# Opening the MLP with plain blocks and keeping its last two pairs on chip

## The chip, the cores and the metric

The kernel runs on one core of one Trainium2 chip. The metric is device time in microseconds (us) of one execution; the time before is 2349.77 us, the median of three runs (2349.01 to 2350.35). Two more figures belong to the one execution that the profiler recorded: its own time, 2352.8 us, and its span, 2351.0 us from the first to the last instruction.

## What is computed

Two encoder layers over 1152 tokens (1024 of a prompt, 8 x 16 of later chunks), width 1024, all in float32. Each layer is a mixer followed by an MLP with a residual:

```python
def channel_mlp(x, w1, w2):
    return jnp.square(jax.nn.relu(x @ w1)) @ w2
...
        yp = yp + mp
        ...
        yp = yp + channel_mlp(rms_norm(yp, ffn_norm_g[layer]), ffn_w1[layer], ffn_w2[layer])
```

`w1` is 1024 x 4096 and `w2` 4096 x 1024. The mixer of layer 0 is attention beside a recurrent branch, that of layer 1 a gated MLP over 128-token chunks; each ends in an output projection of 1024 x 1024 and a residual. The change lies in the MLPs and in the two output projections ahead of them.

## The kernel before

Activations stand with features on the partitions and tokens along the row: eight tiles `x[0]` to `x[7]` of 128 x 1152. TensorE takes float32 in a rounded form, so every operand is split into a high and a low part: ScalarE copies the high part (`split_to` for activations, L390; L189 for weights), VectorE subtracts it from the value (L391, L190). Each product is three matmuls, high-high, high-low, low-high (`product`, L1228, matmul at L1235), on two stretches of 288 tokens.

**The MLP's products** are made from blocks of 2 x 2 with seven products in place of eight (Winograd's form of Strassen's scheme), numbered 1 to 7. In the first product (`first_product`, L1240) a *pair* m, of 16, is the two slabs m and m+16 of `w1`, 128 outputs each; its blocks are the two slabs by the two halves of the inputs (tiles 0-3, 4-7), and the activations are cut into the same halves and into token halves t1 and t2 of 576. One product of a pair is 4 x 2 x 3 = 24 matmuls and is called a *step*. The activations' seven operands `B[1]` to `B[7]` are made once: `B[1]` and `B[2]` are blocks of the first token half as they are, `B[3]` one of the second, and 6, 5, 7, 4 are sums and differences (`other_operands`, L1153). The weights' sums are made pair by pair on VectorE (`Weights.source`, L159), then split into one of 7 slots (`W_SLOTS`), one per step (`W.pump`). Results gather in PSUM banks of the tag `two`, of which there are four, and go by ScalarE or VectorE to rows `c`.

**What follows a pair** goes into the deque `post`, three entries after each step: relu and square on ScalarE, four differences on VectorE (L1261), and seven stores (L1253): each splits one block into a tile `ho` and sends 576 KB to `hidden` in DRAM, since the second product needs its seven operands in split form.

**The second product** (`second_product`, L1325) runs over 8 groups g of two pairs, and for each over two halves q of the outputs, so k = 2g+q counts 0 to 15; each k has 14 steps of 12 matmuls. A group needs 14 tiles `h`, read back from `hidden`; they stand in a ring of 17 slots that also holds three `x` tiles, and group g+1 is loaded as group g is used up. VectorE adds every step's result to `x` (L1352). The residual `x` was put aside in `scratch` by the output projection and is read back at the start (`x_load`, L1076).

**Ahead of the MLP** the output projection (`out_projection`, L1129; `out_bank`, L1091) makes one bank of 128 x 384 at a time, d the output tile and nb the third of the tokens, adds it to `x`, stores it in `scratch`, and sums the squares for the RMS norm with `stat` (L443): ScalarE squares, GpSimd or VectorE adds (L456). The last nine banks are d = 5, 6, 7 for each nb, and the sums are made at those. `normalise` takes the sums over partitions with TensorE (`stat_tokens`, L466), runs the reciprocal root as a chain of small VectorE operations (`rsqrt`, L430), spreads the result with TensorE (`spread_stat`, L476) and scales the eight tiles (`scale`, L1116). For nb = 1 this is called one bank late, after bank (5,2), and followed by the splits of `B[1]` and `B[2]`. For nb = 2 it runs inside the first product, in `last_statistics` and `other_operands`, which then makes all five other operands in one go after the third step.

The first product starts with these steps (m, n); `B[3]` is wanted at the fourth:

```python
        todo = [(0, 1), (0, 2), (1, 1), (0, 3), (1, 2), (0, 6), (0, 5), (1, 3), (0, 7), (1, 6), (0, 4), (1, 5), (2, 1), (1, 7),
                (2, 2), (1, 4)]
```

It ends with pairs 14 and 15 together; then `mlp` (L1383) empties `post`, closes the operands' space, opens the ring, which lies in that space, and only then are the first loads of `h` asked for. All large transfers are issued by SyncE (the rows' SPq), which takes them in its own order. The compiler may set the order of each engine's instructions other than the program does where they do not depend on one another.

Of the kernel before, what the change touches and what calls it, by code (L numbers as in the profile page):

```python
# [19 lines left out]
P = 128  # L20
# [19 lines left out]
W_SLOTS, WX_SLOTS = 7, 5  # L40

PRODUCTS = (1, 2, 4, 6, 5, 7, 3)
H_SLOTS = 17
# [54 lines left out]
class Weights:  # L98
# [5 lines left out]
    def __init__(self, nc, raw_pool, pools, order):  # L104
# [14 lines left out]
        self.raw, self.tiles, self.s2 = {}, {}, None  # L119
# [13 lines left out]
    def _needs(self):  # L133

        last = {}
        for i, (key, n, first, how) in enumerate(self.ops):
            if how is None or n in (1, 2, 7, 3):
                last[first] = i
            if how is not None and n in (4, 5, 6, 3):
                last[first + 1] = i  # L140
        return last
# [17 lines left out]
    def source(self, i):  # L159

        key, n, first, how = self.ops[i]
        if how is None:
            return self.raw[first][:, n * 512:n * 512 + 512]
        r0, r1 = self.raw[first], self.raw.get(first + 1)
        a11, a12 = r0[:, 0:512], r0[:, 512:1024]
        if n in (1, 2, 7):
            return a12 if n == 2 else a11
        v = self.nc.vector
        if n == 3:
            v.tensor_sub(a12, a12, self.s2)  # L170
            return a12
        a21, a22 = r1[:, 0:512], r1[:, 512:1024]
        if n == 6:
            v.tensor_sub(a11, a11, a21)
            v.tensor_add(a21, a21, a22)
            v.tensor_sub(a22, a22, a11)
            self.s2 = a22
        return {4: a22, 6: a22, 5: a21}[n]
# [92 lines left out]
def body(ctx, tc, io):  # L271
# [79 lines left out]
    def add_mlp(l):  # L351
        for m in range(FP):
            order.append((("w1", l, m), [io["w1"][l, m], io["w1"][l, m + FP]], PRODUCTS))
        for g in range(FP // 2):
# [88 lines left out]
    def stat(nb, kt, src, on_dve=False, sum_on_dve=False):  # L443
        if kt == 0:
            s = space["st"].pool.tile([P, NBW], F32, tag="s", bufs=space["sums"], name=f"s{stat.n}")
# [630 lines left out]
    def x_load(d, src, tag=None):  # L1076
        if tag == "h":
            x[d] = space["ring"].pool.tile([P, NTOK], F32, tag="h", bufs=H_SLOTS, name=f"x{d}_{x_load.n}")
# [12 lines left out]
    def out_bank(key, keep, kts=range(KT), ps=None):  # L1091
# [34 lines left out]
    def b_tile(name, n):  # L1126
        B[n] = space[name].pool.tile([P, 2, 4, HT], F32R, name=f"b{n}_{Phase.n}")

    def out_projection(key, keep, gi):  # L1129
# [8 lines left out]
        while todo:  # L1138
            out_bank(key, keep)
            if todo and todo[0] == (6, 1):  # L1140
                normalise(0, gi)
            if todo and todo[0] == (6, 2):
                normalise(1, gi)
                for kt in range(4):
                    b_split(1, kt, x[kt][:, 0:HT])
                for kt in range(4):
                    b_split(2, kt, x[kt + 4][:, 0:HT])
        psum(two=1)

    def last_statistics(gi):  # L1150
        stat_tokens(NB - 1, "two")

    def other_operands(gi):  # L1153

        spread_stat(NB - 1, "two")
        scale(NB - 1, gi)
        for k in sorted((k for k in ("st", "xn0", "xn1")), key=lambda k: -space[k].n):
            space.pop(k).close()
        space["rest"] = Phase("rest")
        for n in (3, 4, 6, 5, 7):  # L1160
            b_tile("rest", n)
        t1, t2 = slice(0, HT), slice(HT, NTOK)
        for kt in range(4):
            b_split(3, kt, x[kt + 4][:, t2])
        for kt in range(4):
            u, v = x[kt], x[kt + 4]
            nc.vector.tensor_sub(u[:, t1], u[:, t2], u[:, t1])
            nc.vector.tensor_sub(u[:, t2], v[:, t2], u[:, t2])
            nc.vector.tensor_sub(v[:, t2], v[:, t2], u[:, t1])
            b_split(6, kt, v[:, t2])  # L1170
        for kt in range(4):
            b_split(5, kt, x[kt][:, t1])
            b_split(7, kt, x[kt][:, t2])
        for kt in range(4):
            v = x[kt + 4]
            nc.vector.tensor_sub(v[:, t1], v[:, t1], v[:, t2])
            b_split(4, kt, v[:, t1])
# [61 lines left out]

    def first_product(l, gi):  # L1240

        rows, bk, post = {}, {}, deque()

        def squares(m, n):
            r = rows[m]
            if n == 0:
                post.append(lambda: nc.scalar.activation(r[0], r[0], AF.Relu))
                post.append(lambda: nc.scalar.square(r[0], r[0]))
            else:
                post.append(lambda: nc.scalar.activation(r[1][:, t2], r[1][:, t2], AF.Relu))  # L1250
                post.append(lambda: nc.scalar.square(r[1], r[1]))

        def store(m, n, src):  # L1253
# [4 lines left out]
            post.append(go)  # L1258

        def less(o, a, b):  # L1260
            post.append(lambda: nc.vector.tensor_sub(o, a, b))  # L1261

        def step(m, n):
            if m not in rows:
                rows[m] = []
                for i, tag in enumerate({0: ("xc", "xb"), 1: ("xb", "xb"), FP - 1: ("xc", "xb")}.get(m, ("xa", "xa"))):
                    pool, bufs = (space["early"].pool, 1) if tag == "xc" else (xp, 4)
                    rows[m].append(pool.tile([P, NTOK], F32, tag=tag, bufs=bufs, name=f"c{l}_{m}_{i}"))
            r = rows[m]
            apart = m < 2  # L1270
            b = {1: "x", 6: "x", 7: "x", 4: "x", 2: "y", 5: "z", 3: "w" if apart else "z"}[n]
            first = n in (1, 2, 5) or (apart and n == 3)
# [7 lines left out]
            o = {1: r[0][:, t1], 2: r[0][:, t1], 6: r[0][:, t2], 3: r[0][:, t2], 5: r[1][:, t2], 7: r[1][:, t2], 4: r[1][:, t1]}[n]  # L1280
            o, ps = halved(o), both(ps)
            if n in (1, 5) or n == (3 if apart else 6):
                nc.scalar.copy(o, ps)  # L1283
            elif n == 4:
                nc.scalar.activation(o, ps, AF.Relu)
            else:
                nc.vector.tensor_add(o, ps, o)  # L1287
            if apart and n == 5:
                o = halved(r[0][:, t2])
                nc.vector.tensor_add(o, ps, o)  # L1290
            if n == 4:
                u, v = r
                squares(m, 0)
                store(m, 1, u[:, t1])
                less(u[:, t1], u[:, t2], u[:, t1])
                squares(m, 1)
                store(m, 2, v[:, t1])
                less(u[:, t2], v[:, t2], u[:, t2])
                store(m, 3, v[:, t2])
                less(v[:, t2], v[:, t2], u[:, t1])  # L1300
                store(m, 6, v[:, t2])
                store(m, 5, u[:, t1])
                store(m, 7, u[:, t2])
                less(v[:, t1], v[:, t1], v[:, t2])
                store(m, 4, v[:, t1])

        todo = [(0, 1), (0, 2), (1, 1), (0, 3), (1, 2), (0, 6), (0, 5), (1, 3), (0, 7), (1, 6), (0, 4), (1, 5), (2, 1), (1, 7),
                (2, 2), (1, 4)]
        for m in range(2, FP - 2):
# [359 lines left out]
```

## Time and profile before

| what | value |
| --- | --- |
| median of three runs | 2349.77 us |
| the profiled execution, its own time | 2352.8 us |
| its span | 2351.0 us |
| TensorE busy, matmuls | 2192.3 us (93%) |
| VectorE busy | 1665.6 us (71%) |
| ScalarE busy | 982.2 us (42%) |
| bytes moved by DMA | 406.80 MB |

In the profile, PE is the matmul row of TensorE, PEld its weight loads, DVE VectorE, ACT ScalarE, POOL GpSimd, SP SyncE. A busy share is an average over stages with different limits. A matmul's own duration overlaps the next one's, so the pace of a stretch is its length by its number of matmuls. A row of the windows view gives the stretch from start to end, its length, then busy time and number of instructions (x) of each engine, the clock granted to TensorE as a share of full speed, the DMA engines' busy share and GB/s. In a group row, "busy" is the time covered by the group, and the mean is that of one instruction, which overlaps its neighbour's.

### The profile page before, as it was taken

How to read it: one execution, taken by the hardware profiler on the slowest of the kernel's cores; microseconds unless marked ns; L12 is line 12 of the kernel's file. 1: busy time of each engine (PE TensorE's matmuls, PEld its weight loads, DVE VectorE, ACT ScalarE, POOL GpSimd, SP SyncE). 2: the span in 40 equal slices, each digit the busy share in tenths (PEclk: the TensorE clock that was granted, in tenths of full speed). 3: DMA queues.
4: the chain of work that ended last, by engine and by line, in shares of the span. 5: the costliest groups of instructions: out<-in, count | busy, mean ns of one | idle time of the engine just before them, and what ended most of it. 6: DMA issues, size and time to landing. Idle time of an engine off the chain costs nothing.

```text
span 2351.0 us, 38871 instructions
## 1 busy us (share of the span) xinstructions
PE 2192.3 (93%) x15348; PEld 2156.7 (92%) x15348; DVE 1665.6 (71%) x2900; ACT 982.2 (42%) x1768; POOL 275.6 (12%) x341
## 2 busy tenths in 40 slices
PE   7988989789999949999999999987999995999999
PEld 7977889789999949999999999987999994999999
DVE  7869983878777657777783644278777765777776
ACT  5755662357666521111252213135666653121211
POOL 4256531100000000000050232020000000000000
PEclk9999999899999979999999999998999997999999
DMA  4110043127656596766761013311666667767565
GB/s 148 59 52 5 21 131 98 39 87 285 257 217 239 204 349 227 263 219 215 254 216 37 19 54 101 121 49 57 251 261 236 228 244 284 262 246 259 196 237 195
DMA packets 114918, 406.80 MB, mean 173 GB/s; under 512 B 14240, under 2 KB 25504, under 8 KB 114720
## 3 DMA queue, kind: packets, MB, share of 16 engines
q1 hardware_dynamic: 114592, 404.31, 47.9%
q8 instruction: 121, 1.98, 0.3%
q14 instruction: 61, 0.50, 0.1%
q10 hardware_dynamic: 144, 0.02, 0.0%
HBM read 252.41 MB, written 152.77 MB: 172 GB/s over the span
## 4 chain that ended last, share of the span: by engine, by line
PE 77%; DVE 14%; DMA 4%; ACT 3%; issue 2%; SPq 0%; POOL 0%; ACTq 0%; DVEq 0%; POOLq 0%
PE two L1235 57%; PE mm L509 4%; PE mm L508 4%; PE mm L507 4%; DVE st L246 2%; DMA hidden<-ho 2%; DVE m L246 1%; PE mm L1479 1%; PE mm L1477 1%; PE mm L1478 1%; DVE b L391 1%; PE mm L246 1%; DMA h<-hidden 1%; DVE w L190 1%; DVE x L1116 1%
## 5 line engine op out<-in xcount | busy, mean ns | idle before, releaser
L1235 PE MATMUL two<-h,w 128*128 128x288 f32 x5376 | 725.9, 297 | 61.8 <-DMA h<-hidden 60.6
L1235 PEld LDWEIGHTS two<-h,w 128*128 128x128 f32 x5376 | 724.1, 190 | 63.6 <-issue 40.8
L1235 PE MATMUL two<-b,w 128*128 128x288 f32 x5376 | 736.9, 299 | 36.5 <-ACT b L390 30.2
L1235 PEld LDWEIGHTS two<-b,w 128*128 128x128 f32 x5376 | 730.6, 191 | 42.5 <-ACT b L390 33.0
L189 ACT CAST w<-raw 128x512 fp32r<-128x512 f32 x548 | 338.0, 620 | 761.2 <-PE two L1235 550.0
L190 DVE TENSOR_TENSOR w<-raw,w 128x512 fp32r<-128x512 f32 x548 | 380.3, 696 | 123.5 <-ACT w L189 119.2
L1352 DVE TENSOR_TENSOR x<-two,x 128x576 f32<-128x576 f32 x448 | 337.8, 755 | 166.2 <-PE two L1235 162.0
L391 DVE TENSOR_TENSOR ho<-c,ho 128x576 fp32r<-128x576 f32 x224 | 166.6, 755 | 87.2 <-ACT ho L390 86.4
L390 ACT CAST ho<-c 128x576 fp32r<-128x576 f32 x224 | 143.2, 673 | 50.4 <-DMA hidden<-ho 38.9
L507 PE MATMUL mm<-xn0h,w 128*128 128x384 f32 x372 | 129.2, 347 | 6.7 <-ACT xn0h L503 6.5
L508 PE MATMUL mm<-xn1l,w 128*128 128x384 f32 x372 | 125.9, 339 | 1.3 <-DVE xn1l L504 1.3
L508 PE MATMUL mm<-xn0l,w 128*128 128x384 f32 x372 | 126.8, 341 | 0.0
L509 PE MATMUL mm<-xn0h,w 128*128 128x384 f32 x372 | 126.5, 340 | 0.0
L507 PE MATMUL mm<-xn1h,w 128*128 128x384 f32 x372 | 125.9, 339 | 0.0
L509 PE MATMUL mm<-xn1h,w 128*128 128x384 f32 x372 | 125.7, 338 | 0.0
L1409 POOL TENSOR_TENSOR s<-s,tmp 128x384 f32<-128x384 f32 (+1 forms) x28 | 28.5, 1046 | 770.4 <-DVE x L1352 758.6
L1283 ACT COPY c<-two 128x576 f32<-128x576 f32 x96 | 61.2, 637 | 92.5 <-PE two L1235 91.8
L1287 DVE TENSOR_TENSOR c<-two,c 128x576 f32<-128x576 f32 x96 | 72.4, 754 | 37.4 <-PE two L1235 37.3
L507 PEld LDWEIGHTS mm<-xn0h,w 128*128 128x128 f32 x372 | 71.8, 193 | 8.1 <-ACT xn0h L503 7.1
L1103 DVE TENSOR_TENSOR x<-mm,x 128x384 f32<-128x384 f32 x48 | 26.7, 555 | 65.1 <-PE mm L509 65.1
L508 PEld LDWEIGHTS mm<-xn0l,w 128*128 128x128 f32 x372 | 71.9, 193 | 0.5 <-DVE xn0l L504 0.4
L508 PEld LDWEIGHTS mm<-xn1l,w 128*128 128x128 f32 x372 | 70.6, 190 | 1.6 <-DVE xn1l L504 1.6
(252 smaller groups left out, 2722.6 us busy)
## 6 DMA issues: line engine op xcount, KB each, us to landing
hidden<-ho SPq DMA_DIRECT2D x224, 576.0 KB, 3.2
h<-hidden SPq DMA_DIRECT2D x224, 576.0 KB, 5.9
raw<-in_w SPq DMA_DIRECT2D x128, 512.0 KB, 4.3
x<-scratch SPq DMA_DIRECT2D x24, 576.0 KB, 6.6
scratch<-x SPq DMA_DIRECT2D x48, 192.0 KB, 1.8
raw<-in_wo SPq DMA_DIRECT2D x16, 512.0 KB, 3.6
xin<-in_xT SPq DMA_DIRECT2D x24, 192.0 KB, 4.2
x<-in_xT SPq DMA_DIRECT2D x8, 576.0 KB, 6.1
```

Of the source, the lines that this page charges most:

```text
L189: nc.scalar.copy(t[:, 0], src)
L190: nc.vector.tensor_sub(t[:, 1], src, t[:, 0].bitcast(F32))
L246: return lambda *a, **k: self.tc.keep_in_program_order(op(*a, **k))
L390: nc.scalar.copy(hi, src)
L391: nc.vector.tensor_sub(lo, src, hi.bitcast(F32))
L507: nc.tensor.matmul(ps, wh, ah, start=start, stop=False)
L508: nc.tensor.matmul(ps, wh, al, start=False, stop=False)
L509: nc.tensor.matmul(ps, wl, ah, start=False, stop=stop)
L1235: nc.tensor.matmul(o, w, a[:, c], start=first and k == 0 and i == 0, stop=k == len(pairs) - 1 and i == 2, skip_group_check=True)
L1283: nc.scalar.copy(o, ps)
L1287: nc.vector.tensor_add(o, ps, o)
L1352: nc.vector.tensor_add(o, both(ps), o)
```

## The change

*The start.* Pairs 1 and 2 begin, each with products 1 and 2. Pair 0 is then made by plain blocks: eight steps, first the four on the first token half, which need only `B[1]` and `B[2]`, then the four on the second, which need `B[3]` and a new operand `B[8]` (tiles 0-3, second half). Its weights are loaded as plain slabs (`w1c`), with no sums, and its relu is taken as the result leaves PSUM. The operands of the others are no longer made in one go but dealt out, four entries after each step from the second on. `B[4]` takes the place of `B[8]`. Early rows of pairs 0 to 2 stand in two `xc` tiles and in slots of `xa` and `xb` as these come free (`EARLY`). Slabs 1, 2, 14 and 15 are loaded twice.

*Ahead of it.* `normalise` for nb = 0 and 1 is called as soon as the third's last bank is done. Sums of squares for nb = 0 and 1 are made at each bank of its own tile, from the first on, those of d = 6 and 7 on VectorE; for nb = 2, five at (4,2) and one at each later bank.

*The end.* The seven stores of pairs 14 and 15 split into tiles that stay (`hl`, 12 slots where `B[5]`, `B[4]`, `B[3]` stood, and two of `xa`), and their work waits in a deque of its own, taken up one entry per step in the second product. That product takes its groups in the order 0, 1, 7, 2 to 6, so the kept group is the third. The ring becomes two pools, `hx` (10, where `B[1]`, `B[2]`, `xc` stood) and `hy` (8, where `B[6]`, `B[7]` stood), opened three steps from the end of the first product, where group 0 and the residual are asked for.

*Weights.* The slots are 6 and 6 in place of 7 and 5, and the order of a pair's operands is 1, 2, 7, 6, 5, 3, 4, with the same four sums per pair.

```diff
-W_SLOTS, WX_SLOTS = 7, 5
-PRODUCTS = (1, 2, 4, 6, 5, 7, 3)
-H_SLOTS = 17
+W_SLOTS, WX_SLOTS = 6, 6
+PRODUCTS = (1, 2, 7, 6, 5, 3, 4)
+GROUPS = [0, 1, FP // 2 - 1] + list(range(2, FP // 2 - 1))
+SLOTS = {"hx": 10, "hy": 8, "hl": 12, "xa": 4, "xb": 4}
...
+        order.extend(first[1:3] + [(("w1c", l, 0), [w1[0]], None), (("w1c", l, 1), [w1[FP]], None)] + rest[1:3])
...
-        if d >= 5:
-            for k in ((0, 1, 4, 5), (2, 6), (3, 7))[d - 5]:
-                stat(nb, k, x[k][:, cols], sum_on_dve=nb == NB - 1)
+        if nb < NB - 1 or d >= 4:
+            for k in range(0 if (nb, d) == (NB - 1, 4) else d, d + 1):
+                stat(nb, k, x[k][:, cols], sum_on_dve=d >= (5 if nb == NB - 1 else 6))
...
-            if todo and todo[0] == (6, 1):
-                normalise(0, gi)
-            if todo and todo[0] == (6, 2):
-                normalise(1, gi)
...
+            if todo and todo[0][1] == nb + 1 and todo[0][0] == 5:
+                normalise(nb, gi)
...
+        out = [lambda kt=kt: scale1(kt) for kt in range(KT)]
+        add = lambda fn, *a: out.append(lambda: fn(*a))
+        add(operands)
+        for kt in range(4):
+            add(b_split, 8, kt, x[kt][:, t2])
+        for kt in range(4):
+            add(b_split, 3, kt, x[kt + 4][:, t2])
...
+        add(b_tile, "rest", 4)
         for kt in range(4):
             v = x[kt + 4]
...
+            add(sub, v[:, t1], v[:, t1], v[:, t2])
+            add(b_split, 4, kt, v[:, t1])
+        return deque(out)
...
+        def by_blocks(row, half, j):
...
+            w = W.op(("w1c", l, row), j)
+            n = ((1, 2), (8, 3))[half][j]
+            ps = bk["c"]
+            product(ps, [(w[:, 0, k * P:k * P + P], w[:, 1, k * P:k * P + P], B[n][:, 0, k], B[n][:, 1, k]) for k in range(4)],
+                    j == 0, j == 1)
...
+            if j:
+                nc.scalar.activation(halved(cell(0, f"{row + 1}{half + 1}")), both(ps), AF.Relu)
...
+        todo = [(1, 1), (1, 2), (2, 1), (2, 2)]
+        todo += [(0, row, half, j) for half in range(2) for row in range(2) for j in range(2)]
+        todo += [(1, n) for n in (6, 5, 7, 3)] + [(2, 6), (1, 4)] + [(2, n) for n in (5, 7, 3)] + [(3, 1), (2, 4)]
...
+            if i == 0:
+                last_statistics()
+            elif i == 1:
+                prep = other_operands(gi)
+            for _ in range(4):
+                if prep:
+                    prep.popleft()()
             W.pump(1)
...
+            if t == (b, 7):
+                assert not post
+                space.pop("high").close()
+                space.pop("early").close()
+                for k in ("hx", "hy"):
+                    space[k] = Phase(k, side="right")
+                second_loads(l)
+        return late_post, kept
...
+    def second_loads(l):
...
+        free.extend(["hx"] * (SLOTS["hx"] - 4) + ["hy"] * SLOTS["hy"])
+        for i, n in enumerate(USE):
+            h_load(l, GROUPS[0], n)
+            if i < 2:
+                for d in (2 * i, 2 * i + 1):
+                    x_load(d, scratch[2 * l], "hx")
+        for d in range(4, KT):
+            x_load(d, scratch[2 * l], "xb")
...
+            if k == 4 and not any(key[0] == groups - 1 for key in h):
+                assert not post
+                h.update({(groups - 1, n, p): t for (p, n), t in kept.items()})
+                free.extend(["xa"] * (SLOTS["xa"] - 2))
             step(k, *s)
...
+            if post:
                 post.popleft()()
```

More of the change, by code (lines that the diff above doesn't have):

```diff
@@ L444, in stat @@
         if kt == 0:
-            s = space["st"].pool.tile([P, NBW], F32, tag="s", bufs=space["sums"], name=f"s{stat.n}")
+            if nb == NB - 1 and "early" in space:
+                s = space["early"].pool.tile([P, NBW], F32, tag="xc", bufs=2, name=f"s{stat.n}")
+            else:
+                s = space["st"].pool.tile([P, NBW], F32, tag="s", bufs=space["sums"], name=f"s{stat.n}")
             stat.n += 1
@@ L1076, in x_load @@
     def x_load(d, src, tag=None):
-        if tag == "h":
-            x[d] = space["ring"].pool.tile([P, NTOK], F32, tag="h", bufs=H_SLOTS, name=f"x{d}_{x_load.n}")
+        if tag == "hx":
+            x[d] = space["hx"].pool.tile([P, NTOK], F32, tag="hx", bufs=SLOTS["hx"], name=f"x{d}_{x_load.n}")
         else:
@@ L1238, in body, with cell, whole, act @@
     t1, t2 = slice(0, HT), slice(HT, NTOK)
+    CELLS = {"11": ("a", 0), "12": ("a", 1), "21": ("b", 0), "22": ("b", 1)}
+    EARLY = {0: {"11": ("xc", 0), "12": ("xc", 1), "21": ("xb", 0), "22": ("xb", 1)},
+             1: {"11": ("e", 0), "12": ("a", 0), "21": ("b", 0), "22": ("a", 1)},
+             2: {"11": ("e", 1), "12": ("a", 0), "21": ("b", 0), "22": ("a", 1)}}
     def first_product(l, gi):
[L1242 to L1253, printed above, removed]
-            def go():
+        tiles, bk, post, kept, late_post = {}, {}, deque(), {}, deque()
+        last = (FP - 2, FP - 1)
+        def cell(m, c):
+            name, half = EARLY.get(m, CELLS)[c]
+            key = name if name == "e" else (m, name)
+            if key not in tiles:
+                tag = {"xc": "xc", "e": "xc", "xb": "xb"}.get(name, "xa")
+                pool, bufs = (space["early"].pool, 2) if tag == "xc" else (xp, 4)
+                tiles[key] = pool.tile([P, NTOK], F32, tag=tag, bufs=bufs, name=f"c{l}_{m}_{name}")
+            return tiles[key][:, half * HT:half * HT + HT]
+        def whole(m, name):
+            return tiles[m, name]
+        def act(fn, o):
+            nc.scalar.activation(o, o, AF.Relu) if fn == "relu" else nc.scalar.square(o, o)
+        def store(todo, m, n, src):
+            def go():
+                if m in last:
+                    tag = "hl" if len(kept) < SLOTS["hl"] else "xa"
+                    o = ring_tile(tag, f"hk{l}_{m}_{n}")
+                    kept[m - last[0], n] = o, tag
+                    split_to(o[:, 0], o[:, 1], src)
+                    return
                 o = xp.tile([P, 2, HT], F32R, tag="xb", bufs=4, name=f"ho{l}_{m}_{n}")
@@ L1257, in go @@
                 nc.sync.dma_start(hidden[l][m, n - 1], o.rearrange("p i x -> p (i x)").bitcast(F32))
-            post.append(go)
-        def less(o, a, b):
-            post.append(lambda: nc.vector.tensor_sub(o, a, b))
-        def step(m, n):
[L1264 to L1272, printed above, removed]
+            todo.append(go)
@@ L1357, in step @@
                 W.pump(1)
-                if q == 1 and g + 1 < groups:
-                    load(g + 1, n)
-        use = (1, 2, 6, 5, 7, 3, 4)
-        for n in use:
-            load(0, n)
-            if n == 1:
-                for d in (0, 1):
-                    x_load(d, scratch[2 * l], "h")
-            elif n == 6:
-                x_load(2, scratch[2 * l], "h")
-                x_load(3, scratch[2 * l], "xb")
+                if q == 1:
+                    free.extend(tag for _, tag in (h.pop((g, n, p)) for p in range(2)) if tag != "hl")
+                    while waiting and len(free) >= 2:
+                        h_load(l, *waiting.popleft())
         todo = [(0, 1, 0), (0, 1, 1)]
```

224 lines of the change are left out of this document (132 added, 92 removed).

## The prediction, made before the result

> **What bounds the kernel now.** I read the page first.
>
> ```profile
> span 2351.0 us, 38871 instructions
> ...
> PE 2192.3 (93%) x15348; PEld 2156.7 (92%) x15348; DVE 1665.6 (71%) x2900; ACT 982.2 (42%) x1768; POOL 275.6 (12%) x341
> ...
> PE 77%; DVE 14%; DMA 4%; ACT 3%; issue 2%; SPq 0%; POOL 0%; ACTq 0%; DVEq 0%; POOLq 0%
> ```
>
> TensorE carries 77% of the chain that ended last; what an edit can win is the rest. The timeline of TensorE gives its pace, the windows say where it is not held.
>
> ```profile
> 564.72 261.86 PE L1235 MATMUL two<-b,w 128*128 128x288 f32 x1962 [0.76 <-ACT c L1283]
> ```
>
> ```profile
> core 0: us, PE busy (x) PEld busy (x) DVE busy (x) ACT busy (x) POOL busy (x), PEclk, DMA share, GB/s
> 438.00:492.00 54.00, 35.43 (x202) 32.38 (x201) 51.72 (x92) 25.66 (x43) 0.00 (x0) 0.81 0.06 18
> 826.00:876.00 50.00, 18.28 (x107) 17.65 (x106) 25.38 (x36) 12.71 (x20) 0.00 (x0) 0.66 0.94 360
> 890.00:1180.00 290.00, 290.00 (x2177) 290.00 (x2177) 221.69 (x324) 55.92 (x90) 0.00 (x0) 1.00 0.67 239
> 1566.00:1621.00 55.00, 36.51 (x200) 33.90 (x201) 51.18 (x91) 25.39 (x43) 0.00 (x0) 0.79 0.06 17
> 1956.00:2008.00 52.00, 23.33 (x145) 22.58 (x145) 27.91 (x40) 12.51 (x20) 0.00 (x0) 0.70 0.96 365
> ```
>
> The pace is 261.86/1962 = 0.1335 us a matmul, so a step of 24 takes 3.20 us and one of 12 takes 1.60. In the long stretch, 890 to 1180, the count times the pace is the length: there nothing but fewer matmuls helps. Four stretches fall short: each opening of an MLP (54 - 202 x 0.1335 = 27.0 us and 55 - 26.7 = 28.3) and each passage from first to second product (50 - 14.3 = 35.7 and 52 - 19.4 = 32.6). Together 123.6 us, half clock included; that is all this change can reach. The two kinds have different limits: VectorE is busy 51.72 of 54 us in the opening, while DMA is at 0.94 to 0.96 in the passage. Waits and chain name the releasers.
>
> ```profile
> PE two L1235 <- DMA h<-hidden: 60.6, 6, 29.3
> PE two L1235 <- ACT b L390: 30.2, 12, 5.4
> ```
>
> ```profile
> 830.56 4.74 DMA hidden<-ho
> ...
> 852.39 6.47 DMA x<-scratch
> 858.92 11.38 DMA h<-hidden
> ```
>
> The last pairs' stores drain through DRAM, then the residual comes back, then the first group, all with TensorE idle.
>
> **The passage.** The change removes from it the 14 stores of pairs 14 and 15 and the wait for space: `hx` lies on operands whose last reader, step (15,2), is ten steps ahead of the end. Ten steps are 32 us. Wanted are 14 tiles of group 0 and 8 of `x`.
>
> ```profile
> h<-hidden SPq DMA_DIRECT2D x224, 576.0 KB, 5.9
> ```
>
> ```profile
> 865.00:875.00 10.00, 8.05 (x50) 7.83 (x49) 5.90 (x9) 1.24 (x2) 0.00 (x0) 0.83 1.02 412
> ```
>
> A tile of 576 KB is 0.59 MB, 22 are 13 MB, 31.5 us at 412 GB/s. In the same 32 us go 4.1 MB of pair 13's stores and 1 MB of weights, 12.5 us. So about 13 tiles are there at the end, and the rest follow at 1.4 us each while a product that needs two of them lasts 3.2 us: just in time. If SyncE reaches the loads only at its program place, three steps (9.6 us) from the end, six tiles stand at the end and the next product's come about 1 us late. Transfers cost me 2 us a passage.
>
> What moves in is the work after pairs 14 and 15: two times 15 entries, one per step, 22 of them with a VectorE operation (14 stores, 8 differences), over 30 steps or 48 us.
>
> ```profile
> L391 DVE TENSOR_TENSOR ho<-c,ho 128x576 fp32r<-128x576 f32 x97 | 72.1, 754 | 32.6 <-ACT ho L390 32.2
> L190 DVE TENSOR_TENSOR w<-raw,w 128x512 fp32r<-128x512 f32 x97 | 66.3, 686 | 27.7 <-ACT w L189 27.7
> L1287 DVE TENSOR_TENSOR c<-two,c 128x576 f32<-128x576 f32 x40 | 30.1, 754 | 14.3 <-PE two L1235 14.3
> ```
>
> In the second product VectorE is busy 221.69 of 290 us, 0.764; the entries add 22 x 0.743 = 16.3 us over 48, 0.34. At 1.10 VectorE is the bound for 48 us and falls 5 behind. Four PSUM banks let TensorE run ahead by about two steps' reading, so some of the five stay hidden, and waits of VectorE on ScalarE's halves of the same entries give as much back; behind those waiting subtractions are queued the additions to `x` that free the banks, which TensorE waits for. I take 4. Left of the passage: 6 us, bounds 1 and 16 (the eight `h` of a late queue at 1.4 us, plus 5). Won: 35.7 + 32.6 - 12 = **56.3 us**.
>
> **The opening.** Added on TensorE: one product per layer, 24 x 0.1335 = 3.2 us, on the path. The first wait shrinks:
>
> ```profile
> 408.89 0.56 DVE L1103 TENSOR_TENSOR x<-mm,x 128x384 f32<-128x384 f32 x1 [3.60 <-PE mm L509]
> 413.05 0.56 DVE L1103 TENSOR_TENSOR x<-mm,x 128x384 f32<-128x384 f32 x1 [3.60 <-PE mm L509]
> 413.61 0.16 DVE L468 TENSOR_SCALAR small<-ax 128x3 f32<-128x3 f32 x1
> ...
> 414.81 0.98 DVE L436 SCALAR_TENSOR_TENSOR small<-rT 128x3 f32<-128x3 f32 x1
> ...
> 417.30 0.16 DVE L438 SCALAR_TENSOR_TENSOR rT<-small,rT 128x3 f32<-128x3 f32 x1
> ```
>
> ```profile
> 440.20 0.40 PE L1235 MATMUL two<-b,w 128*128 128x288 f32 x1 [1.88 <-ACT b L390]
> 442.49 0.61 PE L1235 MATMUL two<-b,w 128*128 128x288 f32 x1 [1.89 <-ACT b L390]
> 443.87 1.57 PE L1235 MATMUL two<-b,w 128*128 128x288 f32 x5 [0.77 <-DVE b L391]
> ```
>
> The first three waits are 4.5 us; `normalise(1)` comes one bank (4.16 us) earlier, which removes most of them, and about 2 stay. Then eight steps, 25.6 us, need only `B[1]` and `B[2]`; before, the fourth step wanted `B[3]`. But VectorE still has to make every operand, one more than before. Its operations from the last bank to the 22nd step, (3,1), at these rows:
>
> ```profile
> 438.83 4.31 DVE L1116 SCALAR_TENSOR_TENSOR x<-x,gt,rstd 128x384 f32<-128x384 f32 x8
> ```
>
> ```profile
> L391 DVE TENSOR_TENSOR b<-x,b 128x576 fp32r<-128x576 f32 x28 | 19.3, 752 | 0.1
> ```
>
> Splits of eight operands 32 x 0.69 = 22.1; 16 differences of that size 11.0; scaling 4.3; the root's chain (413.61 to 417.46, 3.9) and its copy (about 0.6, like L1103) 4.5; 20 weight splits x 0.684 = 13.7; 9 weight sums of that size 6.2; 6 bank readings x 0.75 = 4.5; 20 operations of `post` for pairs 0 and 1 x 0.743 = 14.9. Sum 81.2 us, against 22 x 3.20 = 70.5 us of TensorE. VectorE stays the bound by 10.7 us, and TensorE cannot get far ahead: rows of pairs 0 and 1 stand in slots that `x[0]` and `x[4]` hold until `B[7]` and `B[4]` have taken them, so a bank's copy on ScalarE waits there with the operand copies queued behind it, and the next product on that bank behind both. Left: 10.7 + 2, I take 13, bounds 6 (work of `post` slipping behind the 22nd step) and 27 (nothing won). Won: 27.0 + 28.3 - 2 x (13 + 3.2) = **22.9 us**.
>
> **Ahead of it and elsewhere.** Sums of squares per bank put about as many additions on GpSimd as before, but earlier, some beside the end of the attention; one costs 1.05 us (below, two in 2.10), so 0 to 8 us, I take 1. They may not touch the chain of the root: the row at 414.81 takes 0.98 where its like takes 0.16, while this ran:
>
> ```profile
> 414.75 2.10 POOL L456 TENSOR_TENSOR s<-s,tmp 128x384 f32<-128x384 f32 x2 [1.47 <-ACT tmp L454]
> ```
>
> The Trainium skill's page "SBUF — State Buffer", section "Who interferes with whom", has the rule: a VectorE instruction with two SBUF inputs and a GpSimd instruction that reads SBUF exclude each other for a whole instruction. The trace agrees (0.98 against 0.16). By that rule the added early sums could cost VectorE up to their own length as well, some 2 us more in all; by the rows, where TensorE still has a bank to work on, nothing.
>
> Six weight slots for seven: a chunk of the gMLP's weights changes four times, with two tiles ready in place of three; bound 0 to 1.3 us each (ScalarE's cast, about as long as L190's 0.686, then L190), I take 1.5 in all. Slabs loaded twice are 8 x 0.5 MB on DMA engines that the long stretch keeps 0.67 busy: nothing. The kept group means fewer loads in the second product: nothing, as TensorE does not wait there.
>
> **The sum** is made against the profiled execution, 2352.8 us: 2352.8 - 56.3 - 22.9 + 2.5 = 2276.1. It lies 3.0 above the median of the runs, so I predict **2273 us**.
>
> **Rivals.** (a) The opening wins nothing: VectorE, 96% busy there, only changes the order of its work and what is wanted slips from `B[3]` to `B[4]`. For it: the sum of 81.2 us; against it: eight steps that need nothing new. 2273 + 23 = 2296.
>
> (b) Transfers keep part of the passage. Weight loads asked for behind 13 MB of tiles come after them: if issue begins 9.6 us from the end, the last tile lands 22 us after it, the weights 3 later, when the fifteenth step (22.4 us) wants them already split; with late `h` tiles about 14 us a passage more. 2273 + 28 = 2301. For it: DMA at 0.96 there; against it: two `x` loads that went out early in the old passage. The Trainium skill's page "DMA: Bandwidth & Descriptors", section "Queues, rings and completion order", says that an engine consumes descriptors in ring order; it would put these weights behind the tiles, and no row here shows a weight load overtaking.
>
> (c) Everything hides: 6 us left of an opening, 1 of a passage. 2273 - 14 - 10 = 2249.
>
> (d) Slower. With six slots each split waits for the product that frees its slot, and a product for its split. The margin is four products, 12.8 us; once VectorE is later than that, every product pays cast and subtraction, about 1.3 us. There are 448 products' weights in the MLPs; 60 of them paying is 78 us and eats the gain, 100 give 2273 + 130 = 2403. For it:
>
> ```profile
> ACT w L189 <- PE two L1235: 550.0, 231, 15.2
> ```
>
> Casts do wait for TensorE, up to 15.2 us. Against it: VectorE's load is 1.10 for only 48 us, five late, not 12.8.
>
> (e) No change: loads and operands stay where they were, because the orders of the queues do. 2350.
>
> **How the numbers follow.** Forecast (2255 to 2290) 0.58; (a) 0.17; (b) 0.09; (c) 0.06; (d) 0.06; (e) 0.04. The range leaves out (d), (e) and the outer halves of (a), (b), (c): 2249 to 2308. Faster by over 0.2% (4.7 us, about what a measurement can tell from no change) 0.90; within it 0.04; slower 0.06.
>
> **What would show it.** In the profile after: no wait of TensorE on DMA over some 3 us, and in the first 48 us of the second product VectorE over 95% busy, TensorE a few us short; in the opening the first wait under 3 us, the first eight steps nearly whole, short stalls of TensorE on `b` or on ScalarE's copies from the ninth to the 22nd step, VectorE still near 95%. Wrong if TensorE waits on `h` again (b), if the opening still falls 25 us short (a), or if the long stretches are no longer at 0.1335 us a matmul (d).

## The result, and the profile after

The changed kernel takes 2251.03 us, the median of four runs (2248.54 to 2252.7), against 2349.64 us before in the same comparison: a ratio of 0.9579, with a 95% interval of 0.9563 to 0.9596. It is 98.6 us faster, where 76.8 were forecast. The page of the profile after:

```profile
span 2251.0 us, 38887 instructions
...
PE 2178.3 (97%) x15396; PEld 2145.5 (95%) x15396; DVE 1651.9 (73%) x2884; ACT 978.3 (43%) x1770; POOL 276.6 (12%) x341
...
DMA packets 108007, 377.97 MB, mean 168 GB/s; under 512 B 13472, under 2 KB 24736, under 8 KB 107808
```

TensorE does 48 matmuls more, two steps of 24, and fills 97% of a span that is 100 us shorter. DMA moves 28.8 MB less: 33.0 MB of stores and loads of the kept group, less 4.2 MB of slabs loaded twice. The waits of TensorE that touch the MLP's products, in the changed kernel:

```profile
PE two L1268 <- DVE x L1115: 11.2, 2, 5.6
...
PE two L1268 <- DVE x L1467: 2.1, 2, 1.5
```

A wait on `h` (60.6 us before) is no longer in that list, nor is one on an operand `b` (30.2 us before). One new wait stands at the top: twice, at the start of each MLP, TensorE waits 5.6 us for an addition that reads a bank of the output projection. The windows of the changed kernel show the opening (first three rows) and the passage from first to second product:

```profile
core 0: us, PE busy (x) PEld busy (x) DVE busy (x) ACT busy (x) POOL busy (x), PEclk, DMA share, GB/s
441.00:448.00 7.00, 1.40 (x8) 1.11 (x7) 7.00 (x13) 2.62 (x5) 0.00 (x0) 0.79 0.20 43
448.00:473.00 25.00, 25.00 (x179) 25.00 (x178) 19.73 (x42) 12.54 (x21) 0.00 (x0) 0.92 0.22 68
473.00:518.00 45.00, 45.00 (x340) 45.00 (x339) 42.53 (x66) 30.45 (x49) 0.00 (x0) 1.00 0.42 153
810.00:824.00 14.00, 14.00 (x107) 14.00 (x106) 10.95 (x18) 8.33 (x13) 0.00 (x0) 1.00 1.02 411
824.00:872.00 48.00, 46.54 (x345) 45.83 (x344) 44.45 (x68) 14.43 (x25) 0.00 (x0) 1.00 0.69 254
```

The first product ends at 812.6 us, inside the row 810 to 824: TensorE passes into the second product without a stop, DMA at 1.02 beside it. In the opening, TensorE loses most of its time before 448 us; from then on it is busy throughout, up to 473 at a granted clock of 0.92, and from 473 on at full pace (340 matmuls in 45.00 us).

The stages, worked out from the first and last matmul of each product in the two traces (us; "opened" is the wait before the first product and that product, "passed" is the passage and the second product):

| stage | before | after | difference |
| --- | --- | --- | --- |
| layer 0, up to the projection's last bank | 438.3 | 441.9 | +3.6 |
| layer 0, opened | 388.2 | 370.7 | -17.5 |
| layer 0, passed | 395.8 | 362.9 | -33.0 |
| layer 1, up to the projection's last bank | 343.3 | 340.7 | -2.6 |
| layer 1, opened | 389.5 | 371.1 | -18.4 |
| layer 1, passed | 391.9 | 359.7 | -32.2 |

At 0.1335 us a matmul, the changed first product (2712) needs 362.0 us and the second (2688) 358.9. So 8.7 and 9.1 us are left of the openings, 4.0 and 0.8 of all that follows. The +3.6 can't be pinned down: in other kernels of this study with the same code up to there, the same stage ends anywhere between 438.7 and 442.2 us. But the two kernels that sum the squares in the old way are the earliest of all (438.3 us before, 437.0 in the fourth experiment), so part of it is likely the price of the early sums.

### The profile page after: what moved, and what is told of

Its sections match the earlier page's. It is cut to its first block, busy times and chain, and to the rows that moved or that the text cites. A ratio compares the mean times of both kernels' runs of the same rounds, so it can differ in the third digit from the quotient of the medians.

```text
span 2251.0 us, 38887 instructions
## 1 busy us (share of the span) xinstructions
PE 2178.3 (97%) x15396; PEld 2145.5 (95%) x15396; DVE 1651.9 (73%) x2884; ACT 978.3 (43%) x1770; POOL 276.6 (12%) x341
## 5 line engine op out<-in xcount | busy, mean ns | idle before, releaser
L1268 PE MATMUL two<-b,w 128*128 128x288 f32 x5424 | 728.9, 296 | 11.2 <-DVE x L1115 11.2
L1268 PE MATMUL two<-h,w 128*128 128x288 f32 x4704 | 630.6, 295 | 4.3 <-DVE x L1467 2.1
L1268 PEld LDWEIGHTS two<-h,w 128*128 128x128 f32 x4704 | 627.5, 188 | 6.2 <-issue 3.5
L193 ACT CAST w<-raw 128x512 fp32r<-128x512 f32 x542 | 332.6, 621 | 641.7 <-PE two L1268 442.6
L400 DVE TENSOR_TENSOR ho<-c_a,ho 128x576 fp32r<-128x576 f32 x78 | 57.2, 754 | 46.7 <-ACT ho L399 46.7
L1268 PE MATMUL two<-hk,w 128*128 128x288 f32 x672 | 91.2, 295 | 0.0
L1268 PEld LDWEIGHTS two<-hk,w 128*128 128x128 f32 x672 | 90.1, 188 | 0.0
L1297 ACT ACTIVATE c_a<-c_a 128x1152 f32<-128x1152 f32 x60 | 70.1, 1169 | 15.4 <-DVE c_a L1379 14.6
L1115 DVE TENSOR_TENSOR x<-mm,x 128x384 f32<-128x384 f32 x48 | 26.7, 555 | 66.1 <-PE mm L521 65.9
L400 DVE TENSOR_TENSOR ho<-c_b,ho 128x576 fp32r<-128x576 f32 x96 | 72.4, 754 | 2.2 <-ACT ho L399 2.2
```

What stands on the lines that cost most here:

```text
L193: nc.scalar.copy(t[:, 0], src)
L400: nc.vector.tensor_sub(lo, src, hi.bitcast(F32))
L1115: nc.vector.tensor_add(o, ps[:, :NBW], o)
L1268: nc.tensor.matmul(o, w, a[:, c], start=first and k == 0 and i == 0, stop=k == len(pairs) - 1 and i == 2, skip_group_check=True)
L1297: nc.scalar.activation(o, o, AF.Relu) if fn == "relu" else nc.scalar.square(o, o)
```

## What the new wait is

The four banks of the first product lie where the projection's banks lay, so a product can't start until VectorE has read those. VectorE's timeline at that place, changed kernel:

```profile
439.32 5.43 DVE L400 TENSOR_TENSOR b<-x,b 128x576 fp32r<-128x576 f32 x8
444.67 0.56 DVE L1115 TENSOR_TENSOR x<-mm,x 128x384 f32<-128x384 f32 x1
445.14 1.29 DVE L194 TENSOR_TENSOR w<-raw,w 128x512 fp32r<-128x512 f32 x2
446.34 0.56 DVE L468 TENSOR_TENSOR s<-s,tmp 128x384 f32<-128x384 f32 x1
446.81 0.56 DVE L1115 TENSOR_TENSOR x<-mm,x 128x384 f32<-128x384 f32 x1
```

The projection's last matmul ended near 441.9. The readings of the last two banks (L1115) stand behind eight operand splits and, the last one, behind two weight splits; the last is done at 447.4, and TensorE starts at 447.51. Theory: TensorE waits because the splits of `B[1]` and `B[2]` stand ahead of the readings. Rival: the work is the same, and what goes first doesn't matter.

**First experiment: the splits go behind the readings.** Four splits are made before the last bank, four after all.

```diff
-                if nb == 1:
-                    for kt in range(4):
-                        b_split(1, kt, x[kt][:, 0:HT])
-                    for kt in range(4):
-                        b_split(2, kt, x[kt + 4][:, 0:HT])
+            if nb == NB - 1 and len(todo) == 1:
+                for kt in range(4):
+                    b_split(1, kt, x[kt][:, 0:HT])
         psum(two=1)
+        for kt in range(4):
+            b_split(2, kt, x[kt + 4][:, 0:HT])
```

> The changed kernel with one thing moved: the eight splits of B[1] and B[2] stand behind the reading of the last bank's predecessor (B[1]) and of the last bank (B[2]) in the program, instead of ahead of both. Theory: what is left of the opening's first wait (5.6 us in each MLP) is that the first product's PSUM banks are those of the output projection, whose last two readings are queued on VectorE behind the scaling and the eight splits. Then the wait falls to 1 to 2 us and the half clock behind it goes: 2251 - 2 x 4 to 6 = 2239 to 2243. Rival: TensorE would wait just as long for the splits themselves; then 2249 to 2253, with the wait put down to B.

Measured: 2245.51 us (2241.02 to 2245.79), ratio to before 0.9549 (0.9535 to 0.9563). Its wait of TensorE, and the last part of VectorE's timeline ahead of it:

```profile
PE two L1268 <- DVE x L1115: 5.8, 2, 2.9
```

```profile
440.92 1.28 DVE L194 TENSOR_TENSOR w<-raw,w 128x512 fp32r<-128x512 f32 x2
442.12 0.55 DVE L1115 TENSOR_TENSOR x<-mm,x 128x384 f32<-128x384 f32 x1
```

The wait falls from 5.6 to 2.9 us per layer: the theory stands. The time falls by 5.5 us, less than expected: the last reading still stands behind two weight splits, and half clock still follows the wait (below).

**Eighth experiment: the last reading first.** As the first, and the reading of the last bank is issued ahead of the weight splits (`pump`), all of `B[2]`'s splits after it:

```diff
+        if (d, nb) == (KT - 1, NB - 1):
+            nc.vector.tensor_add(o, ps[:, :NBW], o)
         pump(0, 0, 0, 2)
...
-        nc.vector.tensor_add(o, ps[:, :NBW], o)
+        if (d, nb) != (KT - 1, NB - 1):
+            nc.vector.tensor_add(o, ps[:, :NBW], o)
```

> As the first experiment, with all splits of B[1] and B[2] behind or beside the last bank, and besides the addition that reads the projection's last bank placed ahead of the two weight splits and of the splits of B[2]. Theory (the first product waits for VectorE to free the projection's banks, because readings stand in its queue behind splits): the wait of TensorE for the addition falls from 2.9 to 1 to 2 us per layer and the half-clock period with it, 2240 to 2244. Rival (the wait only moves from the bank to the operands or the weights, which now come later): within 2 us of the first experiment, 2244 to 2248, with a new wait of TensorE on b or w of about the same length.

Measured: 2242.49 us (2241.04 to 2246.34), ratio 0.9546 (0.9528 to 0.9565). Its waits of TensorE, and its start of the product on TensorE's timeline:

```profile
PE two L488 <- DVE rT L447: 5.2, 2, 2.6
...
PE two L1271 <- DVE x L1113: 3.4, 2, 1.7
```

```profile
441.09 3.44 PE L1271 MATMUL two<-b,w 128*128 128x288 f32 x24 [1.71 <-DVE x L1113]
444.37 0.72 PE L478 MATMUL two<-ones,s 128*128 128x1 f32 x6
444.95 3.43 PE L1271 MATMUL two<-b,w 128*128 128x288 f32 x24
450.96 0.93 PE L488 MATMUL two<-ident,rT 128*128 128x128 f32 x6 [2.58 <-DVE rT L447]
```

Both were partly right. The wait for the bank falls to 1.7 us, and 2.6 us of a new one appear after the second step, where TensorE must spread a root that VectorE has not finished. With the half clock that also goes (below), the two openings come to 367.7 us each. They are 370.7 and 371.1 in the changed kernel. This is the fastest version run, 8.5 us under the changed kernel's median; from the first experiment the intervals don't tell it apart.

**Ninth experiment: the spreading one step later,** on top of the eighth: `other_operands` after the third step (`elif i == 2`) instead of the second.

> As the eighth experiment (the last bank's reading first), with the broadcast of the last third's reciprocal roots, and with it the scaling and all operands behind it, one step of 3.20 us later. Theory (TensorE stood 2.6 us per layer at the broadcast only because the chain of the root had not ended, and the operands have a step to spare): that wait goes and nothing takes its place, 3 to 5 us off, 2236 to 2240. Rival (VectorE bounds the opening, so what it starts later it ends later): 2241 to 2245, with waits of TensorE on an operand or on a copy of a bank between the ninth and the 22nd step in its place.

Measured: 2247.17 us (2242.65 to 2249.36), ratio 0.9563 (0.9548 to 0.9577). The rival held in its waits; the time lies 2 us above what it gave. The wait at the spreading is gone, and TensorE waits instead near 490 us for a weight's cast on ScalarE, while VectorE is busy without a break. TensorE's wait in all, and the window of that stop:

```profile
PE two L1271 <- ACT w L193: 5.5, 2, 2.8
```

```profile
486.00:491.00 5.00, 2.33 (x18) 2.10 (x16) 5.00 (x9) 2.55 (x5) 0.00 (x0) 1.00 0.29 118
```

The first products are 2.0 and 1.8 us longer than in the eighth. The stop is about as long as the one that went (2.8 us against 2.6), but half clock follows this one (granted clock 0.71 from 490 to 494 us). So making the spreading later only moved the wait.

## What the opening is worth, part by part

**Third experiment: no blocks.** Pair 0 is made by seven products again, with 24 matmuls fewer per layer; the early `normalise` and the piecewise operands stay (from the sixth step on, all that is left is emitted at once).

```diff
-        todo += [(0, row, half, j) for half in range(2) for row in range(2) for j in range(2)]
-        todo += [(1, n) for n in (6, 5, 7, 3)] + [(2, 6), (1, 4)] + [(2, n) for n in (5, 7, 3)] + [(3, 1), (2, 4)]
+        todo += [(0, 1), (0, 2)] + [(1, n) for n in (6, 5, 7, 3)] + [(2, 6), (1, 4)] + [(2, n) for n in (5, 7, 3)]
+        todo += [(0, 6), (2, 4)] + [(0, n) for n in (5, 7, 3)] + [(3, 1), (0, 4)]
```

> The changed kernel with pair 0 made by its seven products again (products 1 and 2 of pairs 1, 2, 0 first, then 6, 5, 7, 3 of pair 1), no B[8], operands dealt out four per step up to the sixth step and then all. 24 matmuls fewer per layer, 3.2 us. Theory: the plain blocks buy 19 us of work that wants no new operand; without them B[6] is wanted 19 us after the start instead of 38 and VectorE cannot have it: stalls of 12 to 20 us a layer come back, net 2251 + 2 x (9 to 17) = 2269 to 2285. Rival: dealing the operands out is what counts, six steps are enough; then the time falls by the work saved, to about 2245 to 2251.

Measured: 2280.41 us (2279.63 to 2285.09), ratio 0.9706 (0.9692 to 0.9721), 29 us over the changed kernel. The first products are 15.3 and 17.8 us longer, with 3.2 us less to compute, as the theory had it. TensorE's timeline of this kernel shows where:

```profile
475.48 1.85 PE L1265 MATMUL two<-b,w 128*128 128x288 f32 x12 [0.72 <-DVE c_xc L1378]
478.86 0.40 PE L1265 MATMUL two<-b,w 128*128 128x288 f32 x1 [1.52 <-ACT b L399]
480.16 7.92 PE L1265 MATMUL two<-b,w 128*128 128x288 f32 x34 [0.90 <-DVE b L400]
490.92 9.86 PE L1265 MATMUL two<-b,w 128*128 128x288 f32 x72 [2.83 <-ACT c_a L1373]
```

The waits for operands and for copies of banks are back from the seventh step on, and slower matmuls after them: 34 in 7.92 us, where 4.5 would do. The block steps, and the order that they allow, are what won the opening; emitting the rest at the sixth step, which this run also changes, is priced at about 2 us by the fifth experiment.

**Fourth experiment: the old statistics.** Sums and `normalise` as in the kernel before, the rest as changed.

```diff
-        if nb < NB - 1 or d >= 4:
-            for k in range(0 if (nb, d) == (NB - 1, 4) else d, d + 1):
-                stat(nb, k, x[k][:, cols], sum_on_dve=d >= (5 if nb == NB - 1 else 6))
+        if d >= 5:
+            for k in ((0, 1, 4, 5), (2, 6), (3, 7))[d - 5]:
+                stat(nb, k, x[k][:, cols], sum_on_dve=nb == NB - 1)
```

> The changed kernel with the part ahead of the MLP undone: sums of squares at the last nine banks as before, normalise called one bank late. Theory: calling it a bank earlier is worth little as long as the readings of the last banks wait behind the splits, and the sums of squares at each bank slowed the end of the attention in layer 0 by 3.6 us (438.3 to 441.9 us at the last bank); so layer 0's last bank comes 2 to 4 us earlier, the opening starts 2 to 5 us later after it and stalls more, since the statistics of the last third have more additions behind the last bank: 2251 to 2262. Rival: the early call carries much of the opening's gain, as the prediction had it; then each opening loses 4 to 8 us, 2259 to 2267 and no gain in the stage ahead.

Measured: 2252.83 us (2251.05 to 2253.85), ratio 0.9582 (0.9566 to 0.9598), not to be told from the changed kernel. The same wait, longer:

```profile
PE two L1268 <- DVE x L1115: 15.9, 2, 8.0
```

The theory held. The earlier `normalise` is worth 2.4 us of wait per opening, and the openings are 2.6 and 2.8 us longer without it. But layer 0's last bank comes at 437.0 us here, against 438.7 to 442.2 with the early sums, so the early sums may give back what the early call wins; the times don't tell the two apart.

**Fifth experiment: operands in one go.** Of the entries that are dealt out four per step, 41 are emitted after the second step.

```diff
-            for _ in range(4):
+            for _ in range(41 if i == 1 else 4 if i > 10 else 0):
```

> Of the operands, 41 entries are emitted at once after the second step of an MLP, the rest from the twelfth step on four at a time; nothing else differs from the changed kernel. Theory: dealing them out matters, because the bank readings, weight splits and the first evacuations of the product then stand in VectorE's and ScalarE's queues behind some 25 us of operand work. TensorE holds about two steps of banks and three or four products of weights, 6 to 10 us, so it stops for 5 to 15 us per layer: 2260 to 2280, with waits of TensorE on b, w or a bank between the second and the twelfth step. Rival: only the order of the products matters, VectorE has the same sum to do by the 22nd step either way and ends it at the same time: within 3 us of 2251.

Measured: 2255.1 us (2251.98 to 2256.59), ratio 0.9596 (0.9577 to 0.9614). The first products are 2.4 and 1.9 us longer, with 0.8 and 0.7 us of waits for copies of banks (`c_xb`, `c_xc`) that the changed kernel doesn't have. The theory of 5 to 15 us per layer fell; the rival is nearer. Dealing out is worth about 2 us per layer, as far as the stages show it (the times overlap with the changed kernel's): the order of the steps does the rest.

**Seventh experiment: more work for VectorE.** Eight subtractions (the low parts of `B[5]` and `B[7]`) are done twice, 5.5 us per layer.

```diff
+                out[-1] = lambda: (again(), sub(B[n][:, 1, kt], src, B[n][:, 0, kt].bitcast(F32)))
```

> The low part of the operands B[5] and B[7] is computed twice, eight more VectorE operations of 0.69 us per layer, 5.5 us, all within the first 22 steps; nothing else differs. Theory of the prediction (VectorE is the bound of the opening, 81 us of work against 70.5 of TensorE): each microsecond is paid, first product 5 to 6 us longer per layer, 2261 to 2263. Rival (VectorE has some 7 us to spare in the opening, because work of the finished pairs slips behind the 22nd step): 0 to 2 us per layer, 2251 to 2255.

Measured: 2259.18 us (2257.89 to 2260.87), ratio 0.9615 (0.9598 to 0.9632): 8.2 us over the changed kernel, its first products longer by 4.5 and 3.3 us. A new wait in its list:

```profile
PE two L1274 <- ACT c_a L1380: 5.3, 2, 2.7
```

This lies between the two, nearer to the theory. TensorE waits 2.7 us for 5.5 added, so VectorE had about 2.8 us to spare in the changed opening. In layer 0 the half clock after that wait (below) adds most of the rest; in layer 1 there is none, and 0.6 us stay unexplained.

## What the passage is worth, part by part

**Second experiment: the last group is stored and read back after all,** in the old order of groups. The stores stand in the second product, with the late work; the ring is the new one.

```diff
-GROUPS = [0, 1, FP // 2 - 1] + list(range(2, FP // 2 - 1))
+GROUPS = list(range(FP // 2))
...
                     split_to(o[:, 0], o[:, 1], src)
+                    nc.sync.dma_start(hidden[l][m, n - 1], o.rearrange("p i x -> p (i x)").bitcast(F32))
                     return
```

> The changed kernel, but the work of pairs 14 and 15 also stores its fourteen tiles per layer to DRAM as before, the groups run in the order 0 to 7, and the last group is read back; the early loads of group 0 and the dealt-out work behind the last step stay. Theory: the passage is won by asking for group 0 early and by taking the last pairs' work off the way, and that the tiles themselves stay on chip is worth nothing: 2251, within 3 us. Rival: the 14 stores meet the loads of group 0, x and group 1 in the queue, at DMA engines that are full for some 35 us there; then the passage loses 5 to 15 us a layer, 2261 to 2281.

Measured: 2265.24 us (2262.1 to 2266.87), ratio 0.9636 (0.9622 to 0.965), 14 us over the changed kernel; second products 6.7 and 5.7 us longer. The theory fell, the rival held. ScalarE's waits between 805 and 925 us, and TensorE's in all, in this kernel:

```profile
ACT w L193 <- DMA raw<-in_w: 20.4, 2, 16.4
```

```profile
PE two L1268 <- ACT w L193: 8.4, 3, 3.7
```

ScalarE waits up to 16.4 us for weights, and TensorE 3.7 us for ScalarE. The chain of waits of this kernel between 845 and 885 us says what the weights waited for:

```profile
844.74 11.90 DMA hidden<-hk
...
856.66 11.44 DMA hidden<-hk
...
868.16 11.21 DMA raw<-in_w
...
879.47 0.63 ACT w L193
...
880.14 4.93 PE two L1268 x18
```

Store behind store, then the weight load, which SyncE issues only after them and which then takes 11.2 us to land, for 0.5 MB, behind the tiles already under way. In the changed kernel weight loads of that stretch land in 5.1 us (median), ScalarE waits at most 6.8 us for one, and no wait of TensorE there is put down to ScalarE. The Trainium skill's page "DMA: Bandwidth & Descriptors", section "Queues, rings and completion order", has descriptors consumed in ring order; this chain agrees, which no row of the kernel before could show. So keeping the group on chip is worth about 6 us per layer here, the order of the groups that it goes with included.

**Sixth and tenth experiments: the late work twice as fast, and all of it first.** The entries left after pairs 14 and 15 go two per step; in the tenth, all 30 ahead of the second product.

```diff
-            if post:
-                post.popleft()()
+            for _ in range(2):
+                if post:
+                    post.popleft()()
```

> The work after pairs 14 and 15 is put into the second product two entries per step instead of one, 15 steps instead of 30; nothing else differs. By the prediction's step VectorE's load is then 0.764 + 16.3/24 = 1.44 for 24 us, so it falls some 10.6 us behind where one entry per step left it 5 behind. Theory of the prediction (TensorE feels most of what VectorE falls behind): 4 to 7 us more per layer, 2259 to 2265, second product 367 to 370 us. Rival (additions to x and weight splits can lie several us late before TensorE feels it, since four banks and six weight slots cover it): within 3 us of 2251, second products of 360 to 363.

> All the work left after pairs 14 and 15 (30 entries, 22 VectorE operations of 0.743 us, 16.3 us) is put ahead of the second product, against the changed kernel's one entry per step. The sixth experiment showed two per step to cost 1 to 2 us per layer. Theory (TensorE goes on until its four banks are full, about two steps or 6.4 us of reading, and its six weight slots are used, so most of a delay of 16 us reaches it): 8 to 13 us per layer, 2267 to 2277, with waits of TensorE on x or w in the first 24 us of the second product. Rival (the work was as good as free wherever it is put): within 4 us of 2251.

Measured: two per step 2253.31 us (2251.74 to 2254.65), ratio 0.9589 (0.9569 to 0.9609), second products 1.0 and 2.2 us longer: its rival held, but for 1 us in layer 0 (364.1 us, where it gave 363 at most). All first 2272.22 us (2271.35 to 2274.18), ratio 0.9672 (0.9659 to 0.9686), 9.7 and 9.9 us per layer: its theory held. TensorE's timeline of the tenth:

```profile
812.85 9.87 PE L1268 MATMUL two<-h,w 128*128 128x288 f32 x72
832.30 17.92 PE L1268 MATMUL two<-h,w 128*128 128x288 f32 x113 [9.58 <-DVE x L1467]
```

TensorE does six steps of 12 matmuls on what is free, 9.9 us, and then stops for 9.6. So the cover, which the prediction put at about two steps' reading, was six steps here: what VectorE falls behind in the sixth experiment costs TensorE 1 to 2 us a layer, the 16 us of work put ahead in the tenth cost 10.

## Why the prediction was right, and where it was off

The mechanism held: both passages and a large part of both openings went, by the steps named. The large terms were mis-sized, on the side of caution. The forecast for the profiled execution was 76.7 us off it; the stages give 100.1. So 2251 us lies near the lower end of the range of 2249 to 2308, and below the 2255 to 2290 that were given a chance of 0.58.

**Passage: won 65.2, forecast 56.3.** The transfers of a passage were allowed 2 us and cost none that the profile names: no wait of TensorE in the products is put down to DMA. SyncE reached the loads much earlier than the program place, which had been the fear behind the bounds. Its timeline, changed kernel:

```profile
784.35 2.21 SPq L1427 DMA_DIRECT2D h<-hidden  x2
...
797.61 11.96 SPq L1427 DMA_DIRECT2D h<-hidden  x10
```

The first load goes out 28 us before the end of the first product, as the ten steps of free space allowed. VectorE was allowed 4 us. The first 48 us of layer 0's second product:

```profile
812.50:860.50 48.00, 46.54 (x345) 45.83 (x345) 44.12 (x67) 17.50 (x30) 0.00 (x0) 1.00 0.74 285
```

By the prediction VectorE's load was 1.10 here; measured it is 0.92, under the forecast 95%, and TensorE loses 1.46 us (0.72 in layer 1). Of the 1.46 the profile puts 0.38 down to a weight split on VectorE and names nothing for the other 1.08. So the size was wrong, and the place is shown only in part. The bound of rival (b), late weights, needed the stores of the second experiment to come true, and then at 6 to 7 us a passage, not 14.

**Opening: won 35.9, forecast 22.9.** Here the step that failed is "left: 10.7 + 2". The 2 us of the first wait were 5.6, since the prediction had not looked at what stands ahead of the bank readings on VectorE. The 10.7 us of VectorE were none: not one wait of TensorE lies between the first step and the 22nd. In their place came half clock over the first step:

```profile
447.51 5.38 PE L1268 MATMUL two<-b,w 128*128 128x288 f32 x24 [5.60 <-DVE x L1115]
452.72 0.72 PE L478 MATMUL two<-ones,s 128*128 128x1 f32 x6
453.31 3.44 PE L1268 MATMUL two<-b,w 128*128 128x288 f32 x24
```

The first step takes 5.38 us and the second 3.44, so 1.9 us are lost (2.4 in layer 1), and the small matmuls of the statistics between the first three steps take 1.2 us. With the wait these make up the 8.7 and 9.1 us per layer, where 13 were allowed.

Why the sum of 81.2 us was too high can be read from the groups of VectorE in the changed opening, 441.6 to 519 us. Two of the 30 and the window itself:

```profile
L400 DVE TENSOR_TENSOR b<-x,b 128x576 fp32r<-128x576 f32 x29 | 20.7, 758 | 0.0
...
L400 DVE TENSOR_TENSOR ho<-c_xb,ho 128x576 fp32r<-128x576 f32 x4 | 3.0, 756 | 0.5 <-ACT ho L399 0.5
```

```profile
441.60:519.00 77.40, 71.80 (x526) 71.52 (x525) 69.65 (x120) 45.00 (x73) 0.00 (x0) 0.96 0.34 116
```

The groups of that stretch add up to 77.7 us, but VectorE is busy for 69.65: each instruction overlaps the one before it a little, and a group's time leaves that out only where its own instructions follow one another. Eight splits in a row take 5.43 us, 0.68 each; alone, one takes 0.75 to 0.76. The prediction priced mixed work at 0.743, as if each stood alone. The other 3.5 us (81.2 less 77.7) are mainly three splits done before the last bank, the root's chain (2.7 us where 4.5 were taken) and five operations of `post` that slipped behind the 22nd step, less 2.2 us for the last two banks, which the count had missed. That VectorE is still the next limit was right: some 2.8 us to spare (seventh experiment), and nothing won by moving the wait (ninth).

The remaining 4.7 us of the opening were there before and not seen: by the stages the two openings of the kernel before lost 29.4 and 30.6 us, where the windows gave 27.0 and 28.3. The windows' count took small matmuls of the statistics and of the projection for full ones, and a stop near 564 us lay outside them.

**Elsewhere:** +2.5 forecast, +1.0 measured, within the spread of that stage. **Rivals:** (a) is out, TensorE doesn't fall short by 25 us in an opening; (c), 2249 us, is the nearest: its 1 us left of a passage is about what the windows show (1.46 and 0.72), its 6 us of an opening are 9, and the larger losses that the kernel before had make up for that. (d) is out: the long stretches keep their pace, with six slots too:

```profile
600.00:700.00 100.00, 100.00 (x752) 100.00 (x751) 76.13 (x114) 65.53 (x99) 0.00 (x0) 1.00 0.62 233
```

752 matmuls in 100 us are 0.1330 each. (e) is out by the result.

## What to carry to other kernels

Before an operation is moved forward on an engine, look at what it is put in front of: here the splits stand ahead of the additions that free the banks for the next phase, and setting them behind won 2 to 3 us per opening, as much as calling `normalise` a bank earlier did. An order of work that needs fewer operands at first was worth 15 to 18 us per opening, the fine dealing of the same operations 2. To see whether an engine is a bound, take its busy time in the window, not the sum of its groups' times; and to see how much it has to spare, give it more to do.

## What was not expected of the hardware

TensorE's half clock followed some waits of less than three microseconds. Windows of three kernels, in this order: the first experiment (after 2.91 us idle), the seventh (2.65 us), the changed kernel (5.60 us):

```profile
443.20:446.60 3.40, 3.40 (x16) 3.40 (x16) 3.28 (x6) 0.08 (x1) 0.00 (x0) 0.51 0.82 217
```

```profile
499.40:502.80 3.40, 3.40 (x16) 3.40 (x16) 3.40 (x7) 1.03 (x2) 0.00 (x0) 0.52 0.01 2
```

```profile
445.05:451.88 6.83, 4.37 (x18) 4.40 (x19) 3.98 (x8) 1.05 (x2) 0.00 (x0) 0.50 0.69 194
```

The granted clock is 0.50 to 0.52 for 3.4 us or for twice that. In the changed kernel it falls 2.5 us before work starts again at 447.51 us; in the seventh it falls about 1.4 us after (0.96 from 497.90 to 499.40 us). Nothing of the kind follows the 1.71 and 2.58 us of the eighth experiment: 24 matmuls take 3.44 us there. Nor does it follow the seventh's other wait of 2.65 us, in layer 1:

```profile
1550.00:1595.00 45.00, 42.35 (x318) 42.10 (x317) 43.25 (x66) 28.20 (x45) 0.00 (x0) 1.00 0.31 108
```

So the length of a wait alone doesn't decide it; what does isn't shown here. TensorE's first step in the first experiment:

```profile
442.81 4.95 PE L1268 MATMUL two<-b,w 128*128 128x288 f32 x24 [2.91 <-DVE x L1115]
```

So 1.2 us less of waiting saved 1.5 us more in the first step. The Trainium skill's page "TensorE: Matmul & The Clock Gate", section "HAM oscillation — how this bites in real kernels", gives as a rule that no idle gap should be longer than about 3.4 us. As a safe gap that is too long by these rows; 3.4 us is the length of the slow period here, or half of it.
